# Late heads of a hybrid trunk: the norm factor's row, the decays and the last score take other places in the order

## The chip, the cores and the metric

The kernel runs on one core of a Trainium2 chip. The metric is device time in microseconds (us) of one execution. A core has five engines that work side by side, each through its own instructions in order: TensorE (PE in the profile, PEld for its weight loads), VectorE (DVE), ScalarE (ACT), GpSimd (POOL) and SyncE (SP), which here mostly issues DMAs. An instruction that waits holds up everything behind it on its engine.

## What is computed

The reference is a two-layer trunk on a sequence of 512 positions and 2048 features: an mLSTM layer of 8 heads, and then a band-attention layer. Both are modulated by a conditioning vector (the "ada" products). The change touches the mLSTM layer alone. Cut to that:

```python
proj = h @ w_in
qk = silu(causal_conv(proj[..., :A_V0], conv_w, conv_b))
v, o, z = proj[..., A_V0:A_O0], proj[..., A_O0:A_Z0], proj[..., A_Z0:A_G0]
gates = proj[..., A_G0:] + gate_b
ht = mlstm_chunkwise(heads(qk[..., :A_QK]), heads(qk[..., A_QK:]), heads(v), li, lf)
ht = rmsnorm(ht, g_head)
y = (sigmoid(o) * ht * silu(z)) @ w_out
```

Per head, `mlstm_chunkwise` is a causal attention without softmax: scores q·k are multiplied by decays, the exponential of a difference of gate sums, multiplied into the values and divided by a norm; then comes an RMS norm over the head's 512 columns.

## The kernel before

**Products and weights.** All products are in fp32 made of three products of split operands: x = hi + lo, both in the format that PE takes at full speed, and hi·hi + hi·lo + lo·hi. Weights stream from DRAM in numbered pieces of 128 rows by up to 1024 columns. SP loads piece i to `wr`i. ACT casts it to `wh`i (the hi part), then DVE subtracts it from the raw piece (the lo part, same tile): `split`, L243. Where a projection uses fewer products by a Strassen-like scheme, DVE first makes sums of the piece's blocks, `ws`i (L282 to L284, of which L283 writes into the raw piece, so that the cast of `wh`i waits for it), and these are split in turn into `wsh`i. So each piece of a late head costs ACT two casts and DVE five instructions, and PE multiplies `wh` and `wsh` against the activations `h1` and their sums `h1s`.

**Heads.** Heads 0 to 2 run beside the conditioning sums and the build-up of `h1s`. Heads 3 to 7 (h > `HALF`, the late heads) all run alike, 165.9 us each: a pair of projections for the queries (`proj_s` through `pair`, 4 pieces, in head 3 pieces 105 to 108), a pair for the keys (109 to 112), the values (`proj_v`, 8 pieces, 113 to 120), four pairs of output and gate projections (`ps_dzo` and so on, 16 pieces), and then norm, denominator and numerator of the head. Each projection of queries and keys goes through `conv`: an affine step on ACT, three multiply-adds on DVE (L793, written into `cv`), a silu on ACT (L796), and a split into `qk`. `proj_v` runs its 8 pieces (k = 0 to 7, n = 8) against two blocks of positions (b = 0, 1), whose banks `ps_d`, `ps_c`, `ps_a` and a shared `ps_e` are accumulated in PSUM; pieces 0 and 1 are held and run together, block 0 of both and then block 1 of both, and so are the last two, 6 and 7. Behind the last piece's block 0 `empty` reads that block's banks.

**Scores.** `scores(h, j)` for j = 0 to 3 is called amid the values pieces: six products into `ps_s`, two exponentials on ACT (L855, L857) into `e` (the decays; `e` tiles come from a pool that they share with others), a multiplication on DVE (L860) and a split into `p`; for j = 3 a single multiplication (L865). For j > 0 the result is added to a total (L870). Before, score 3 is called before piece 7 is fetched, so it stands on PE amid the held pieces.

**The norm factor's row.** The norm and square sum of a head are known at its end; `row_out` sends them to DRAM and `factor(h)` loads them back as a 16x32 tile `f` with DMAs on POOL (L886). The rest of it is deferred (`head_due`) into the next head: maximum (DVE, L890), square (ACT, L891), a multiply-add and a clamp (DVE, L892, L893), square root (ACT, L894), reciprocal (DVE, L895), then two DMAs on POOL (L896, L897) that spread the row over 128 partitions in `ssum`. Two of the instructions are tied behind `parted[0]`, the subtraction of the last weights piece at that point in the program. A second `head_due` amid the values multiplies the head's output rows by `ssum` (L904).

**What sets the order.** The program is given to a list scheduler, which orders each engine's instructions by priority: program order, moved forward by `tc.high_priority(lead)` by `lead` steps (`AHEAD` is 300). `behind(a, b)` adds an order without a semaphore. ACT keeps one set of function tables at a time; a switch of functions is an instruction of its own, ACT_TABLE_LOAD, under the line of the function that needs it.

Of the kernel before, what the change touches and what calls it, by code (L numbers as in the profile page):

```python
# [10 lines left out]
F32R = mybir.dt.float32r  # L11
AF = mybir.ActivationFunctionType
# [3 lines left out]
P = 128  # L16
D = 2048
S = 512
KT = D // P
NH = 8  # L20
DK = 256
DV = 512
INNER = 4096
V0 = 4096
# [9 lines left out]
AHEAD = 300  # L34
# [10 lines left out]
HEAD_PAIRS = 8  # L45
RAMP = [4, 5, 6, 7]
HALF = 2
# [140 lines left out]
def hybrid_trunk(ctx, tc, xT, xN, c, adaT, cols, wst, wg, ext, kc, out):  # L188
# [233 lines left out]
    def proj_v(mat, xs, ss, zs, name, pl, bufs, at={}):  # L422

        h0, h1_ = slice(0, 256), slice(256, 512)
        E = newp(f"ps_e{name}")
        banks = [[new(f"ps_{n}{name}_{b}") for n, new in zip("dca", news)] for b, news in enumerate(([newp] * 3, [newa, newp, newa]))]
        begun = set()
        n = KT // 2  # L430
        held = []

        def products(b, k, main, extra):
            D, C, A = banks[b]
            tok = slice(b * P, (b + 1) * P)
            for ps, half, parts, blk, x in (
                (D, 1, main, 1, ss[k][1]),
                (D, 0, main, 0, xs[2 * k][:, :, h0]),
                (C, 0, extra, 1, ss[k][2]),
                (C, 1, extra, 0, ss[k][0]),  # L440
                (A, 0, main, 3, xs[2 * k + 1][:, :, h0]),
                (A, 1, main, 2, ss[k][3]),
                (E, b, extra, 2, xs[2 * k + 1][:, :, h1_]),
            ):
                start = id(ps) not in begun
                begun.add(id(ps))
                w = slice(blk * 256, (blk + 1) * 256)
                last = k == n - 1 and (b if ps is E else ps is not D and half or ps is D and not half)
                mm3(ps[:, h1_ if half else h0], x[:, 0, tok], x[:, 1, tok], parts[0][:, w], parts[1][:, w], start, bool(last), 256)

        def empty(b):
            D, C, A = banks[b]
            z0, z1 = zs(b)
            f0, f1 = h0, h1_
            with tc.high_priority(AHEAD):
                nc.scalar.copy(z0[:, f0], D[:, h0])
                nc.vector.tensor_tensor(z1[:, f1], z0[:, f0], D[:, h1_], op=ALU.add)
                nc.vector.tensor_tensor(z1[:, f0], z1[:, f1], C[:, h0], op=ALU.add)
                nc.vector.tensor_tensor(z0[:, f1], z1[:, f1], C[:, h1_], op=ALU.add)
                nc.vector.tensor_tensor(z1[:, f1], z1[:, f0], C[:, h1_], op=ALU.add)  # L460
                nc.vector.tensor_tensor(z0, z0, A, op=ALU.add)
            return z0, z1

        out = []
        for k in range(n):
            if k in at:
                at[k]()
            held.append((k, *wpiece(mat, [2], pl, bufs)))
            if k in (0, n - 2):
                continue  # L470
            for b in range(2):
                for piece in held:
                    products(b, *piece)
                if k == n - 1:
                    out.append(empty(b))
            held.clear()
        for z, e in zip(out, (h0, h1_)):
            with tc.high_priority(AHEAD):
                nc.vector.tensor_tensor(z[1][:, h0], z[1][:, h0], E[:, e], op=ALU.add)
        return [z[a] for a in range(2) for z in out]  # L480
# [299 lines left out]
            nc.tensor.transpose(pt[:, j * 8 : j * 8 + 8], e[:, j * P : (j + 1) * P], ident[:8, :8])  # L780
        nc.vector.tensor_copy(aT.rearrange("p a b -> p (a b)"), pt[:, :32])

    def conv(ps, ch, name, first, woven):

        acc = tp.tile([P, S], F32, tag="t", name=f"cv_{name}")
        with tc.high_priority(AHEAD if first else 0):
            if woven:
                rows = tp.tile([P, S], F32, tag="t", name=f"cu_{name}")
                nc.scalar.copy(like(rows, S), read(ps, S))
# [2 lines left out]
            for d in range(1, 4):  # L792
                nc.vector.scalar_tensor_tensor(  # L793
                    acc[:, d:], ps[:, : S - d], col(CW + 32 * (3 - d) + ch), acc[:, d:], op0=ALU.mult, op1=ALU.add
                )
        nc.scalar.activation(acc, acc, AF.Silu)  # L796
        t = hp.tile([P, 2, S], F32R, tag="qk", name=f"qk_{name}", bufs=4)
        split(t[:, 0, :], t[:, 1, :], acc)
        return t

    def sums(ps, x, name, early=0, late=0):
# [41 lines left out]
    def scores(h, j, qk, pr, nm, nmd, tot):  # L843
# [8 lines left out]
        psn = read(ps[:, : S - t0], S - t0)  # L852
        e = tp.tile([P, S], F32, tag="t", name=f"e{h}_{j}")
        a = aT[:, j, h : h + 1]
        nc.scalar.activation(e[:, 0:P], nmd[:, j, :], AF.Exp, bias=a)  # L855
        if n > P:
            nc.scalar.activation(e[:, P:n], nm[:, P * (j + 1) :], AF.Exp, bias=a)  # L857
        if j < 3:
            with tc.high_priority(AHEAD):
                nc.vector.scalar_tensor_tensor(like(e[:, :n], n), psn, DK**-0.5, like(e[:, :n], n), op0=ALU.mult, op1=ALU.mult)  # L860
# [53 lines left out]
    for h in range(NH):  # L914
# [4 lines left out]
        for i in range(4):  # L919
            if h > HALF:  # L920
                if i % 2 == 0:
                    zs = pair((i // 2) * (V0 // 2) + h * DK, f"zq{h}_{i}", BANKS[i // 2], HEAD_PAIRS, {3: head_due} if i else {}, lead=AHEAD - 30 * i)
                ps = zs[i % 2]
            elif h < 2:
                ps = (lead, qk1)[h][i]
            else:
                ps = newp(f"ps_qk{h}_{i}")
                proj_a("a_w_in", h1, ps)
            qk.append(conv(ps, chs[i], f"{h}_{i}", 1 < h <= HALF, h in (0, HALF)))
            if 1 < h <= HALF:  # L930
                background(2)
                if i in (2, 3):
                    head_due()
# [30 lines left out]
        if h > HALF:  # L964
# [2 lines left out]
                t = [acp.tile([P, S], F32, tag="so", name=f"zv{h}_{b}_{a}", bufs=6) for a in range(2 - b)]  # L967
                return t + [hp.tile([P, S], F32, tag="nm", name=f"v{h}_3")] if b else t

            pv = proj_v("a_w_in", h1, h1s, rows_of, f"v{h}", hq, (2, 2), {k // 2: f for k, f in at.items()})  # L970
        else:
            pv = [newp(f"ps_v{h}_{m}") for m in range(4)]
            proj_b("a_w_in", h1, pv, at=at)
# [728 lines left out]
```

## Time and profile before

| | us |
|---|---|
| three runs | 2643.46 median, 2641.71 to 2646.48 |
| the profiled execution | 2643.82, its span 2642.1 |
| granted TensorE clock in it | 0.997 |
| ACT busy | 1436.6 |
| DMA | 193 GB/s in the mean |

The profile is a list of instructions with start, length, engine, line (L), operation, and tiles written <- read; in brackets stands the idle time of the engine just ahead and what ended it. Shown ends of instructions in a pipeline overlap the next one's start, so costs are read from start to start. The lines that carry the argument stand below.

### The profile page before, as it was taken

The page shows a single profiled execution, that of the slowest core. Times are in us where ns is not written, and L with a number is a line of the kernel's source. Part 1 is how long each engine was busy: PE and PEld are TensorE (multiplying, and loading weights), DVE is VectorE, ACT ScalarE, POOL GpSimd, SP SyncE. Part 2 cuts the span into 40 slices and gives each one's busy share as a digit, 9 for nine tenths or more (in the row PEclk, how much of TensorE's full clock was granted, in tenths as well). Part 3 has the DMA queues.
Part 4 walks back from the last instruction along what each step waited for, and adds up shares of the span by engine and source line. Part 5 has one row for each costly group of instructions (what it writes and reads, how often), then busy time and mean ns, then how long its engine had stood idle before and what let it go on. Part 6 is the DMA issues. An engine that isn't in the chain of part 4 may idle for free.

```text
span 2642.1 us, 45759 instructions
## 1 busy us (share of the span) xinstructions
PE 2575.3 (97%) x17994; PEld 2407.0 (91%) x17994; DVE 2335.6 (88%) x3812; ACT 1436.6 (54%) x2113; POOL 59.5 (2%) x118
## 2 busy tenths in 40 slices
PE   8999998999999999999999999999999999999998
PEld 6887887899999999999999898788999899999887
DVE  8978988999989999899998886977998999999767
ACT  4344533466556565565655443578543666676523
POOL 0000111000000000000000000000000000000000
PEclk9999999999999999999999999999999999999999
DMA  9776787533333323333246648888754544444787
GB/s 365 310 266 239 275 330 281 198 112 109 126 101 123 124 98 133 104 118 126 99 134 221 214 152 303 305 258 302 230 181 139 180 136 133 139 131 132 255 292 257
DMA packets 155314, 510.61 MB, mean 193 GB/s; under 512 B 17893, under 2 KB 31749, under 8 KB 140633
## 3 DMA queue, kind: packets, MB, share of 16 engines
q1 hardware_dynamic: 144346, 443.89, 49.1%
q0 software_dynamic: 10752, 63.79, 6.6%
q8 instruction: 141, 2.31, 0.4%
q14 instruction: 75, 0.61, 0.1%
HBM read 473.96 MB, written 38.90 MB: 194 GB/s over the span
## 4 chain that ended last, share of the span: by engine, by line
PE 56%; DVE 24%; issue 8%; DMA 6%; ACT 5%; POOL 0%; SPq 0%; DVEq 0%; ACTq 0%; POOLq 0%
DVE wh L243 6%; PE ps_y L311 5%; PE ps_dzo L311 4%; PE ps_czo L311 4%; PE ps_azo L311 4%; DVE ada L550 3%; PE ps_cz L311 3%; PE ps_dz L311 3%; PE ps_y_True L311 3%; PE ps_y_False L311 3%; PE ps_az L311 3%; DMA wr<-in_wst 2%; PE ps_bzo L311 2%; DVE wsh L243 2%; DVE cv L793 2%
## 5 line engine op out<-in xcount | busy, mean ns | idle before, releaser
L243 ACT CAST wh<-wr 128x1024 fp32r<-128x1024 f32 (+1 forms) x536 | 553.1, 1033 | 456.0 <-DVE wr L283 94.3
L243 DVE TENSOR_TENSOR wh<-wr,wh 128x1024 fp32r<-128x1024 f32 (+1 forms) x536 | 642.4, 1201 | 130.5 <-ACT wh L243 129.5
L243 ACT CAST wsh<-ws 128x768 fp32r<-128x768 f32 (+1 forms) x296 | 241.7, 817 | 308.5 <-PE ps_az L311 66.5
L243 DVE TENSOR_TENSOR wsh<-ws,wsh 128x768 fp32r<-128x768 f32 (+1 forms) x296 | 276.3, 933 | 49.1 <-ACT wsh L243 48.2
L550 DVE CUSTOM_DVE_ANT_0 ada<-ada,scB,cl 128x2048 f32<-128x2048 f32 (+1 forms) x89 | 205.7, 2320 | 12.5 <-DMA ada<-in_adaT 12.5
L282 DVE TENSOR_TENSOR ws<-wr 128x512 f32<-128x512 f32 (+1 forms) x296 | 197.6, 669 | 5.0 <-DMA wr<-in_wst 4.7
L311 PE MATMUL ps_y_False<-wh,y 128*128 128x512 f32 x768 | 168.4, 380 | 2.4 <-DVE wh L243 2.4
L311 PE MATMUL ps_y<-wh,y 128*128 128x512 f32 x768 | 168.6, 381 | 0.2 <-DVE wh L243 0.2
L311 PEld LDWEIGHTS ps_y_False<-wh,y 128*128 128x128 f32 x768 | 144.2, 189 | 24.4 <-DVE wh L243 4.3
L311 PEld LDWEIGHTS ps_y<-wh,y 128*128 128x128 f32 x768 | 144.3, 189 | 20.9 <-DVE wh L243 0.6
L311 PE MATMUL ps_v<-wh,h 128*128 128x512 f32 x576 | 129.2, 383 | 0.0
L311 PE MATMUL ps_kv<-wh,hkv 128*128 128x512 f32 x576 | 127.1, 381 | 1.7 <-DVE wh L243 0.9
L311 PEld LDWEIGHTS ps_kv<-wh,hkv 128*128 128x128 f32 x576 | 108.0, 189 | 18.4 <-DVE wh L243 2.4
L284 DVE TENSOR_TENSOR ws<-wr 128x256 f32<-128x256 f32 (+1 forms) x296 | 121.4, 412 | 3.4
L311 PEld LDWEIGHTS ps_v<-wh,h 128*128 128x128 f32 x576 | 109.4, 191 | 16.3 <-issue 0.9
L283 DVE TENSOR_TENSOR wr<-ws,wr 128x256 f32<-128x256 f32 (+1 forms) x296 | 121.0, 411 | 2.5
L311 PE MATMUL ps_l<-h,wh 128*128 128x512 f32 x480 | 107.8, 380 | 2.7 <-DVE wh L243 2.1
L311 PEld LDWEIGHTS ps_l<-h,wh 128*128 128x128 f32 x480 | 90.2, 189 | 17.4 <-DVE wh L243 3.3
L311 PE MATMUL ps_azo<-h,wh 128*128 128x256 f32 (+1 forms) x606 | 92.9, 285 | 0.0
L311 PE MATMUL ps_y_True<-wh,y 128*128 128x512 f32 x384 | 83.6, 380 | 0.3 <-ACT y L1250 0.3
L311 PEld LDWEIGHTS ps_y_True<-wh,y 128*128 128x128 f32 x384 | 72.5, 189 | 10.9 <-ACT y L1250 0.7
L311 PEld LDWEIGHTS ps_azo<-h,wh 128*128 128x128 f32 x606 | 79.3, 192 | 1.1
(432 smaller groups left out, 5827.2 us busy)
## 6 DMA issues: line engine op xcount, KB each, us to landing
wr<-in_wst SPq DMA_DIRECT2D x506, 512.0 KB, 3.7
ada<-in_adaT POOLq DMA_DIRECT2D x57, 1024.0 KB, 7.4
ada<-in_adaT SPq DMA_DIRECT2D x49, 1024.0 KB, 7.5
ada<-in_adaT SPq DMA_DIRECT2D x36, 512.0 KB, 6.7
wr<-in_wst SPq DMA_DIRECT2D x26, 384.0 KB, 5.3
xt<-nsc SPq DMA_DIRECT2D x32, 256.0 KB, 3.6
yr<-ysc SPq DMA_DIRECT2D x28, 256.0 KB, 5.3
ysc<-zo SPq DMA_DIRECT2D x24, 256.0 KB, 3.9
```

The source lines that it names most:

```text
L243: ins = nc.scalar.copy(hi, src), nc.vector.tensor_tensor(lo, src, hi.bitcast(F32), op=ALU.subtract)
L282: nc.vector.tensor_tensor(t[:, : 2 * w], r[:, w : 3 * w], r[:, : 2 * w], op=ALU.subtract)
L283: nc.vector.tensor_tensor(r[:, w : 2 * w], t[:, w : 2 * w], r[:, :w], op=ALU.add)
L284: nc.vector.tensor_tensor(t[:, 2 * w :], r[:, 3 * w :], r[:, w : 2 * w], op=ALU.subtract)
L311: product[0] = nc.tensor.matmul(ps, a, b, start=start, stop=stop)
L550: pin(nc.vector.tensor_tensor_reduce(c, c, (sc or scB)[:, j * w : (j + 1) * w], 1.0, mod[:, i : i + 1] if j else col(CB + i), ALU.mult, AL ...
L793: nc.vector.scalar_tensor_tensor(acc[:, d:], ps[:, : S - d], col(CW + 32 * (3 - d) + ch), acc[:, d:], op0=ALU.mult, op1=ALU.add)
```

## The change

Four things in the diff:

1. In late heads the deferred rest of the norm factor is called at step 1 instead of step 3 of the keys' pair of four pieces (`{1: head_due}`).
2. In `conv` the silu and the split of its result now stand inside the high-priority block. The parameter `first` becomes `lead`: `AHEAD` in head 2 as before, 100 for the keys of late heads, and 0 elsewhere.
3. In late heads the exponentials of `scores` are ordered behind the last convolution's silu (`silu[0]`).
4. `proj_v` calls the function due at step n behind block 0 of the last two pieces and their `empty`; score 3 of late heads is moved to that step.

```diff
@@ proj_v
                 if k == n - 1:
                     out.append(empty(b))
+                    if b == 0 and n in at:
+                        at[n]()
             held.clear()
@@
-    def conv(ps, ch, name, first, woven):
+    silu = [None]
+
+    def conv(ps, ch, name, lead, woven):
 
         acc = tp.tile([P, S], F32, tag="t", name=f"cv_{name}")
-        with tc.high_priority(AHEAD if first else 0):
+        with tc.high_priority(lead):
...
-        nc.scalar.activation(acc, acc, AF.Silu)
-        t = hp.tile([P, 2, S], F32R, tag="qk", name=f"qk_{name}", bufs=4)
-        split(t[:, 0, :], t[:, 1, :], acc)
+            silu[0] = nc.scalar.activation(acc, acc, AF.Silu)
+            t = hp.tile([P, 2, S], F32R, tag="qk", name=f"qk_{name}", bufs=4)
+            split(t[:, 0, :], t[:, 1, :], acc)
         return t
@@ scores
-        nc.scalar.activation(e[:, 0:P], nmd[:, j, :], AF.Exp, bias=a)
+        decays = [nc.scalar.activation(e[:, 0:P], nmd[:, j, :], AF.Exp, bias=a)]
         if n > P:
-            nc.scalar.activation(e[:, P:n], nm[:, P * (j + 1) :], AF.Exp, bias=a)
+            decays.append(nc.scalar.activation(e[:, P:n], nm[:, P * (j + 1) :], AF.Exp, bias=a))
+        if h > HALF:
+            for ins in decays:
+                behind(ins, silu[0])
@@ the loop over heads
-                    zs = pair(..., {3: head_due} if i else {}, lead=AHEAD - 30 * i)
+                    zs = pair(..., {1: head_due} if i else {}, lead=AHEAD - 30 * i)
...
-            qk.append(conv(ps, chs[i], f"{h}_{i}", 1 < h <= HALF, h in (0, HALF)))
+            qk.append(conv(ps, chs[i], f"{h}_{i}", AHEAD if h == HALF else 100 if h > HALF and i > 1 else 0, h in (0, HALF)))
...
-            pv = proj_v("a_w_in", h1, h1s, rows_of, f"v{h}", hq, (2, 2), {k // 2: f for k, f in at.items()})
+            pv = proj_v("a_w_in", h1, h1s, rows_of, f"v{h}", hq, (2, 2), {k // 2 + (k == KT - 2): f for k, f in at.items()})
```

DVE in the keys' pair of head 3, before (tile names carry the head and the piece, and behind those a running number of the tile):

```order
L243 TENSOR_TENSOR wh109_5045<-wr109_5039,wh109_5045 128x1024
L282 TENSOR_TENSOR ws110_0_5095<-wr110_5093 128x512
L283 TENSOR_TENSOR wr110_5093<-ws110_0_5095,wr110_5093 128x256
L284 TENSOR_TENSOR ws110_0_5095<-wr110_5093 128x256
L243 TENSOR_TENSOR wsh109_0_5048<-ws109_0_5041,wsh109_0_5048 128x768
L243 TENSOR_TENSOR wh110_5099<-wr110_5093,wh110_5099 128x1024
```

And with the change:

```order
L243 TENSOR_TENSOR wh109_5045<-wr109_5039,wh109_5045 128x1024
L282 TENSOR_TENSOR ws110_0_5103<-wr110_5101 128x512
L897 TENSOR_TENSOR f2_4782<-f2_4782 16x32
L283 TENSOR_TENSOR wr110_5101<-ws110_0_5103,wr110_5101 128x256
L899 SCALAR_TENSOR_TENSOR f2_4782<-f2_4782 16x32
L284 TENSOR_TENSOR ws110_0_5103<-wr110_5101 128x256
L900 TENSOR_SCALAR f2_4782<-f2_4782 16x32
L902 RECIPROCAL f2_4782<-f2_4782 16x32
L243 TENSOR_TENSOR wsh109_0_5048<-ws109_0_5041,wsh109_0_5048 128x768
L243 TENSOR_TENSOR wh110_5107<-wr110_5101,wh110_5107 128x1024
```

The four DVE steps of head 2's norm factor (`f2`; lines are seven higher in the changed kernel) now stand among pieces 109 and 110.

ACT in the values of head 3, before, where those steps stood until now:

```order
L791 ACTIVATE cv_3_3_5279<-zq3_2_1_5034,cl_100 128x512
L855 ACT_TABLE_LOAD
L855 ACTIVATE e3_0_5530<-nmd3_5289,aT_1513 128x128
L891 ACTIVATE f2_4782<-f2_4782 16x32
L857 ACTIVATE e3_0_5530<-nm3_5288,aT_1513 128x384
L243 CAST wh116_5475<-wr116_5469 128x1024
L243 CAST wsh115_0_5416<-ws115_0_5409 128x768
L894 ACT_TABLE_LOAD
L894 ACTIVATE f2_4782<-f2_4782 16x32
L243 CAST wsh116_0_5478<-ws116_0_5471 128x768
L796 ACT_TABLE_LOAD
L796 ACTIVATE cv_3_2_5270<-cv_3_2_5270 128x512
```

And with the change:

```order
L795 ACTIVATE cv_3_3_5279<-zq3_2_1_5034,cl_100 128x512
L243 CAST wh116_5475<-wr116_5469 128x1024
L243 CAST wsh115_0_5416<-ws115_0_5409 128x768
L243 CAST wsh116_0_5478<-ws116_0_5471 128x768
L800 ACTIVATE cv_3_2_5270<-cv_3_2_5270 128x512
```

The decays of score 0, the norm factor's square and root, and three loads of function tables are gone from this place.

PE in the last two values pieces of head 3, before (pieces 119 and 120, block 0):

```order
L311 MATMUL ps_av3_0_5295<-wh119_5681,h1_13_1127 128x256 x3
L311 MATMUL ps_s3_3_5687<-qk_3_0_5021,qk_3_2_5276 128x256 x3
L311 MATMUL ps_s3_3_5687<-qk_3_1_5030,qk_3_3_5285 128x256 x3
L311 MATMUL ps_av3_0_5295<-wh119_5681,h1s6_42_4300 128x256 x3
L311 MATMUL ps_ev3_5292<-wsh119_0_5684,h1_13_1127 128x256 x3
```

And with the change:

```order
L311 MATMUL ps_av3_0_5295<-wh120_5693,h1_15_1314 128x256 x3
L311 MATMUL ps_av3_0_5295<-wh120_5693,h1s7_42_4530 128x256 x3
L311 MATMUL ps_ev3_5292<-wsh120_0_5696,h1_15_1314 128x256 x3
L311 MATMUL ps_s3_3_5749<-qk_3_0_5021,qk_3_2_5276 128x256 x3
L311 MATMUL ps_s3_3_5749<-qk_3_1_5030,qk_3_3_5285 128x256 x3
L311 MATMUL ps_dv3_1_5296<-wh119_5681,h1s6_42_4300 128x256 x3
```

Score 3 of head 3 stood amid piece 119 of block 0; it now stands between block 0 and block 1 of both pieces.

More of the change, by code (lines that the diff above doesn't have):

```diff
@@ L921, in hybrid_trunk @@
                 if i % 2 == 0:
-                    zs = pair((i // 2) * (V0 // 2) + h * DK, f"zq{h}_{i}", BANKS[i // 2], HEAD_PAIRS, {3: head_due} if i else {}, lead=AHEAD - 30 * i)
+                    zs = pair((i // 2) * (V0 // 2) + h * DK, f"zq{h}_{i}", BANKS[i // 2], HEAD_PAIRS, {1: head_due} if i else {}, lead=AHEAD - 30 * i)
                 ps = zs[i % 2]
```

## The prediction

> **What bounds the kernel now.** I read the page first, then the groups of matmuls with the wait ahead of each, then the windows and the rows of one late head. From the page, the span and the busy row:
>
> ```profile
> span 2642.1 us, 45759 instructions
> PE 2575.3 (97%) x17994; PEld 2407.0 (91%) x17994; DVE 2335.6 (88%) x3812; ACT 1436.6 (54%) x2113; POOL 59.5 (2%) x118
> ```
>
> PE is busy 97% of the span, so only about 67 us exist that a reordering could win, and of those only what lies where the change works. The changed heads are 3 to 7. Two groups of their matmuls carry a wait (behind the second bar: idle time ahead, and its releaser):
>
> ```profile
> L311 PE MATMUL ps_cv<-wsh,h1s 128*128 128x256 f32 x240 | 42.1, 279 | 8.8 <-DVE wsh L243 8.8
> L311 PE MATMUL ps_s<-qk,qk 128*128 128x256 f32 x96 | 14.5, 282 | 7.3 <-DVE e L860 7.3
> ```
>
> Over five heads that is 8.8 / 5 = 1.8 us and 7.3 / 5 = 1.5 us a head. PE's rows around the two waits of head 3, whose values run from 637.23 to 681.84:
>
> ```profile
> 647.46 0.28 PE L311 MATMUL ps_cv<-wsh,h1s 128*128 128x256 f32 x1
> 649.49 0.49 PE L311 MATMUL ps_cv<-wsh,h1s 128*128 128x256 f32 x2 [1.75 <-DVE wsh L243]
> ...
> 671.85 0.50 PE L311 MATMUL ps_av<-wh,h 128*128 128x256 f32 x3
> 673.36 0.94 PE L311 MATMUL ps_s<-qk,qk 128*128 128x256 f32 x6 [1.01 <-DVE e L860]
> ...
> 675.47 0.50 PE L311 MATMUL ps_cv<-wsh,h1s 128*128 128x256 f32 x3
> ...
> 681.84 0.83 PE L311 MATMUL ps_dzo<-h1s,wh 128*128 128x256 f32 x6
> ```
>
> Groups of three products start 0.335 us apart where nothing waits (so 0.112 us each; shown ends overlap). From start to start the first wait loses 649.49 − 647.46 − 0.112 = 1.92 us and the second 673.36 − 671.85 − 0.335 = 1.18 us: 3.1 us a head, 15.5 us in five. Behind 675.47 nothing waits: 19 groups of 0.335 make the 6.37 us to 681.84. Now what stands behind both waits (length, then busy time and instructions of PE, PEld, DVE, ACT, POOL; clock, DMA share, GB/s):
>
> ```profile
> 615.00:649.40 34.40, 32.74 (x292) 32.44 (x290) 34.36 (x61) 21.99 (x31) 0.00 (x0) 1.00 0.27 93
> 649.40:671.00 21.60, 21.51 (x184) 21.35 (x185) 21.57 (x37) 13.77 (x21) 1.56 (x3) 1.00 0.63 215
> 637.20:681.80 44.60, 41.83 (x362) 41.19 (x362) 42.61 (x78) 28.56 (x41) 1.56 (x3) 1.00 0.41 139
> ```
>
> **VectorE is the bound of this stage**: 34.36 of 34.40 us and 21.57 of 21.60, while ACT is busy for two thirds. PE outruns DVE through keys and values and waits for whichever split weights DVE has not finished. So I count what DVE no longer does between 615 and the last piece of the values (piece 120), not what ACT saves.
>
> **The change part by part.** *The row of the norm factor.* Its instructions now stand on DVE and ACT at 612 to 615, not at 643 to 650. DVE and ACT there before:
>
> ```profile
> 612.31 0.42 DVE L283 TENSOR_TENSOR wr<-ws,wr 128x256 f32<-128x256 f32 x1
> ...
> 614.22 0.96 DVE L243 TENSOR_TENSOR wsh<-ws,wsh 128x768 fp32r<-128x768 f32 x1 [1.02 <-ACT wsh L243]
> ```
>
> ```profile
> 613.36 0.83 ACT L243 CAST wsh<-ws 128x768 fp32r<-128x768 f32 x1 [2.94 <-issue]
> ```
>
> The same instructions where they stood until now, first on DVE and then on ACT:
>
> ```profile
> 642.97 0.17 DVE L890 TENSOR_TENSOR f<-f 16x32 f32<-16x32 f32 x1
> 643.08 0.73 DVE L793 SCALAR_TENSOR_TENSOR cv<-zq,cl,cv 128x511 f32<-128x511 f32 x1
> ...
> 645.07 0.17 DVE L892 SCALAR_TENSOR_TENSOR f<-f 16x32 f32<-16x32 f32 x1
> 645.17 0.73 DVE L793 SCALAR_TENSOR_TENSOR cv<-zq,cl,cv 128x509 f32<-128x509 f32 x1
> 645.83 0.16 DVE L893 TENSOR_SCALAR f<-f 16x32 f32<-16x32 f32 x1
> 645.91 1.52 DVE L793 SCALAR_TENSOR_TENSOR cv<-zq,cl,cv 128x511 f32<-128x511 f32 x2
> ...
> 649.35 0.33 DVE L895 RECIPROCAL f<-f 16x32 f32<-16x32 f32 x1
> 649.62 0.61 DVE L282 TENSOR_TENSOR ws<-wr 128x512 f32<-128x512 f32 x1
> ```
>
> ```profile
> 644.13 0.21 ACT L891 ACTIVATE f<-f 16x32 f32<-16x32 f32 x1
> ...
> 646.54 1.28 ACT L894 ACT_TABLE_LOAD   x1
> 647.83 0.23 ACT L894 ACTIVATE f<-f 16x32 f32<-16x32 f32 x1
> 647.97 0.81 ACT L243 CAST wsh<-ws 128x768 fp32r<-128x768 f32 x1
> ```
>
> From start to start the row costs DVE 0.11 (643.08 − 642.97) + 0.10 + 0.08 + 0.27 (649.62 − 649.35) = 0.56 us; that leaves the saturated stretch. In its new place the first three fall into DVE's idle 1.02 us before 614.22. On ACT the chain is late: the maximum starts at about 612.31, the square runs to about 612.65, the table load takes 1.28 (to 613.93), the root 0.14 to the next start, so the cast of wsh109, at 613.36 until now, begins at about 614.08. ACT had been idle 2.94 us ahead of it, which hides the rest; 614.08 − 613.36 = 0.72 is not hidden. The reciprocal fits into DVE's longer idle time. DVE therefore starts its part of wsh109 0.72 to 0.73 us later, and from there has no gap to make that up in. So far 0.56 − 0.73 = −0.17 us: **this part alone loses a little**.
>
> A sentence on a price that no row here bears: the Trainium skill, "ScalarE: Activation LUTs", section "What ACT_TABLE_LOAD costs", gives a switch of tables about 1283 ns of load and 1380 ns of drain, 2.66 us in all. The trace agrees with the load (1.28) and shows no drain behind it: the load at 646.54 ends at 647.82 and the root starts at 647.83. By the page's figure the cast would begin at about 615.46, the sum of this head would fall by 1.38 us, and nothing would be won (the second rival's outcome).
>
> *The last score and its decay.* In the order of before ACT computes score 3's decay ahead of the next weights' cast, and PE the score itself in the middle of piece 119. DVE and then ACT there:
>
> ```profile
> 670.17 0.42 DVE L283 TENSOR_TENSOR wr<-ws,wr 128x256 f32<-128x256 f32 x1
> ...
> 671.75 1.22 DVE L243 TENSOR_TENSOR wh<-wr,wh 128x1024 fp32r<-128x1024 f32 x1 [0.70 <-ACT wh L243]
> ...
> 673.22 0.95 DVE L243 TENSOR_TENSOR wsh<-ws,wsh 128x768 fp32r<-128x768 f32 x1
> 674.09 0.42 DVE L243 TENSOR_TENSOR p<-e,p 128x256 fp32r<-128x256 f32 x1
> ```
>
> ```profile
> 670.67 1.05 ACT L243 CAST wh<-wr 128x1024 fp32r<-128x1024 f32 x1
> ```
>
> DVE idles 0.70 us for the cast of wh121, which cannot start before L283 is done at about 670.58. In the new order the addition of a decayed score (L877, a 128x384 form, 0.47 us from start to start) stands between L283 and that wait instead of ahead of it, and the decay no longer precedes the cast on ACT (0.1 us). Some 0.4 of the 0.70 us is filled; bounds 0 and 0.70, and I take 0.4 since the cast's own 1.05 us stays. wsh120 is then complete on DVE at 674.09 + 0.73 − 0.56 − 0.4 = 673.86.
>
> PE: score 3 (six products, 0.67 us) now stands behind block 0 of pieces 119 and 120, so its slot in PSUM has 3.0 us more (nine groups of 0.335) to come free and the wait of 1.18 for score 2's DVE step is gone. What is late next is wsh120: PE would reach its first product (675.47 before) at 675.47 − 0.67 − 1.18 − 0.2 to 0.5 (from the first wait) = 673.1 to 673.4 and waits until 673.86. From there on PE's work is the same 6.37 + 0.67 us, so the output products start at 673.86 + 7.04 = 680.90, against 681.84: **0.94 us a head**. The first wait, for wsh115, shrinks by 0.2 to 0.5 (a third convolution step, 0.66, also moves behind wsh115), but what it gives is eaten at wsh120.
>
> Bounds of a head: 0, if the root or the cast eats the rest, and 3.1, if both waits go. Five heads at 0.94: 4.7 us.
>
> *Silu and split of the convolutions under high priority; decays behind the last silu.* In late heads these are orders on engines with the same instructions; seven table loads fewer in all (113 for 120) are ACT time, and ACT is no bound: nothing. In heads 0 and 1 the scheduler's order changes (the subtractions for split weights come behind conditioning sums, some scores come earlier). I expect new PE waits of 1 to 3 us each there and others gone, some 2 us late in all at the end of head 1's gate. What takes that:
>
> ```profile
> 412.83 2.35 DVE L550 CUSTOM_DVE_ANT_0 ada<-ada,scB,cl 128x2048 f32<-128x2048 f32 x1 [0.62 <-DMA ada<-in_adaT]
> ...
> 418.04 1.28 DVE L1047 TENSOR_TENSOR so<-ps_n,so 128x512 f32<-128x512 f32 x2
> ```
>
> ```profile
> 418.78 3.61 PE L311 MATMUL ps_n<-p,v 128*128 128x512 f32 x11 [4.41 <-DVE so L1047]
> ```
>
> PE waits 4.41 us there for a DVE instruction at the end of a row of sums that wait for their own DMA (0.62). PE arriving 2 us late is covered by the 4.41; if that cover went, it would cost those 2. I take 0, bounds −1 (fewer sums ahead of L1047, one is 2.35) and +3.
>
> Sum: −4.7 + 0 = −4.7 against the profiled execution of 2643.82 (span 2642.1 and 1.7 around it): 2639.1. The median of the three runs, 2643.46, is 0.36 lower, and so would give 2638.8. I say **2639.0**.
>
> **The rivals.**
>
> *Both waits go (0.13).* If ACT's switches of tables, not DVE's work, hold back the casts that DVE follows, then fewer switches free both: 11 to 15.5 us, 2628 to 2632. For it: DVE's only two gaps around (1.02 and 0.70) both end with ACT. Against it: 34.36 of 34.40 us without any gap between them.
>
> *The root's chain costs what it saves (0.17).* The earlier root delays wsh109's cast. Each 0.1 us more on ACT is lost one for one on DVE; at 0.94 more, that is a cast at 615.0, nothing is won: 2643.5, between 2641 and 2646. (The page's drain of 1.38 us, above, would do that; the rows show none.) For it: the chain alternates DVE, ACT, DVE, ACT, DVE, each handover behind other work. Against it: 2.94 us of idle time on ACT ahead.
>
> *Slower: DVE blocked by the row's reload (0.08).* The maximum now stands at about 612.3 on a DVE that runs in order, and every weight split is queued behind it. The row goes through DRAM and back on POOL's queue (the second line: median issue to landing):
>
> ```profile
> 608.60 0.48 POOL L886 DMA_DIRECT2D f<-dsc  x1 [3.34 <-DMA dsc<-row]
> ```
>
> ```profile
> f<-dsc POOLq DMA_DIRECT2D x14, 2.0 KB, 1.8
> ```
>
> 608.60 + 0.48 + 1.8 = 610.9, 1.4 us ahead of the need. A landing later than 613 costs one for one, and from about 614.0 the head is slower than before; for 0.2% (5.3 us, about what a measurement of this kernel can tell from no change) all five heads would need 615.0, 4 us late: 2646 to 2650. Against it: the margin.
>
> *The decays aren't moved* is no rival: the order of instructions shows that they are.
>
> **How the numbers follow.** Forecast 0.62, the rivals 0.13, 0.17 and 0.08. The forecast's own spread is 0.4 to 1.3 us a head (the filled idle time from 0 to 0.7) with −1 to +3 from heads 0 and 1: 2636 to 2644. Low end 2631, in the first rival's lower half; high end 2646, all but the last rival. 0.2% below the median is 2638.2: of the forecast's 0.62 some 0.27 lies below it, with the first rival's 0.13 that is faster 0.40. Slower takes 0.06 of the last rival and 0.01 of the forecast, 0.07; the same is the rest, 0.53.
>
> **What would show it.** In the changed profile, in each late head: the wait of ps_s for e is gone; a wait of 0.3 to 0.8 us stands ahead of ps_cv of the last piece, released by DVE's wsh; DVE is still without idle time through the values; the root's table load stands at 612.6 with the next cast at 614.1; values-start to first output product is 43.7 us for 44.6. Wrong would be: the first wait gone too (rival one), the wsh109 subtraction past 615.5 (rival two), an idle DVE ahead of the row's maximum (rival three), or PE waits between 205 and 425 us that the 4.41 us does not swallow.

## The result and the profile after

The changed kernel takes 2638.42 us in the median of 22 runs (2632.55 to 2641.18), the kernel before 2642.91 us in 22 runs beside it (2635.94 to 2648.66). The ratio is 0.9981, with a 95% interval of 0.9976 to 0.9987: 4.5 us less in the medians, 3.4 to 6.3 us by the interval. The forecast was 2639.0. The page's span and busy row:

```profile
span 2633.4 us, 45758 instructions
PE 2574.4 (98%) x17994; PEld 2407.5 (91%) x17994; DVE 2335.1 (89%) x3812; ACT 1428.7 (54%) x2106; POOL 59.8 (2%) x118
```

DVE's busy time is the same (2335.1 for 2335.6 us): the change moves work, it saves none of it. ACT has 7 instructions less, the table loads. The two groups that carried the waits, after:

```profile
L311 PE MATMUL ps_cv<-wsh,h1s 128*128 128x256 f32 x240 | 42.6, 280 | 9.8 <-DVE wsh L243 9.8
L311 PE MATMUL ps_s<-qk,qk 128*128 128x256 f32 x96 | 13.9, 278 | 0.0
```

The scores' wait of 7.3 us is gone (five times 1.01 us in the late heads, and 2.25 us at 260.81, ahead of them), and the split weights' wait has grown by 1.0 us. PE's rows around them in head 3, whose values now start at 633.72:

```profile
643.79 0.28 PE L311 MATMUL ps_cv<-wsh,h1s 128*128 128x256 f32 x1
645.62 0.49 PE L311 MATMUL ps_cv<-wsh,h1s 128*128 128x256 f32 x2 [1.56 <-DVE wsh L243]
...
669.66 0.28 PE L311 MATMUL ps_cv<-wsh,h1s 128*128 128x256 f32 x1
670.33 0.49 PE L311 MATMUL ps_cv<-wsh,h1s 128*128 128x256 f32 x2 [0.40 <-DVE wsh L243]
...
677.36 0.83 PE L311 MATMUL ps_dzo<-h1s,wh 128*128 128x256 f32 x6
```

From start to start the first wait loses 645.62 − 643.79 − 0.11 = 1.72 us (1.92 before), and the second, now for the last piece's sums, 0.56 us (1.18 before, for the score). From the first values product to the first output product are 677.36 − 633.72 = 43.64 us for 44.61. The experiments are read with this **values length** and with the **period**, the time from one late head's first output product to the next one's: 165.93 us before, 164.95 after. From head 4 on both repeat within 0.05 us in most kernels (the first period is 0.1 longer), while whole executions of one kernel differ by 5 to 17 us in the sets of ten or more.

Five periods give 5 × 0.98 = 4.9 us. The two profiled spans differ by 8.7; of that 637.23 − 633.72 = 3.5 us lie ahead of head 3's values, in the part that the experiments show to vary by itself (below).

DVE with the norm factor's row in its new place, and ACT beside it:

```profile
608.67 0.17 DVE L897 TENSOR_TENSOR f<-f 16x32 f32<-16x32 f32 x1
...
610.68 0.34 DVE L902 RECIPROCAL f<-f 16x32 f32<-16x32 f32 x1 [0.92 <-ACT f L901]
611.40 0.96 DVE L243 TENSOR_TENSOR wsh<-ws,wsh 128x768 fp32r<-128x768 f32 x1 [0.38 <-ACT wsh L243]
```

```profile
609.12 1.28 ACT L901 ACT_TABLE_LOAD   x1
610.42 0.23 ACT L901 ACTIVATE f<-f 16x32 f32<-16x32 f32 x1
610.55 0.81 ACT L243 CAST wsh<-ws 128x768 fp32r<-128x768 f32 x1
```

Counted from the start of the values, DVE begins wsh109 22.32 us ahead (633.72 − 611.40) instead of 23.01 (637.23 − 614.22): 0.69 us late, for an expected 0.73. The root starts 0.02 us after its table load ends. The drain that the Trainium skill adds to a load ("ScalarE: Activation LUTs", section "What ACT_TABLE_LOAD costs") shows here no more than before.

DVE at the end of the values, and the cast of wh121 on ACT:

```profile
666.26 0.42 DVE L283 TENSOR_TENSOR wr<-ws,wr 128x256 f32<-128x256 f32 x1
666.60 0.55 DVE L877 TENSOR_TENSOR e<-e,e 128x384 f32<-128x384 f32 x1
...
667.85 1.22 DVE L243 TENSOR_TENSOR wh<-wr,wh 128x1024 fp32r<-128x1024 f32 x1 [0.37 <-ACT wh L243]
669.00 0.42 DVE L867 SCALAR_TENSOR_TENSOR e<-ps_s,e 128x256 f32<-128x256 f32 x1
669.33 0.95 DVE L243 TENSOR_TENSOR wsh<-ws,wsh 128x768 fp32r<-128x768 f32 x1
670.20 0.42 DVE L243 TENSOR_TENSOR p<-e,p 128x256 fp32r<-128x256 f32 x1
```

```profile
666.76 1.06 ACT L243 CAST wh<-wr 128x1024 fp32r<-128x1024 f32 x1 [2.35 <-DVE wr L283]
```

The addition to the total (L877) now stands between L283 and wh121. The idle time ahead of wh121 is 0.37 us (0.70 before), and wsh120 starts 35.61 us behind the values' start for 35.99: 0.38 us earlier.

### The profile page after: what moved, and what is told of

It is laid out like the page before. It is cut to its first block, busy times and chain, and to the rows that moved or that the text cites. A ratio compares the mean times of both kernels' runs of the same rounds, so it can differ in the third digit from the quotient of the medians.

```text
span 2633.4 us, 45758 instructions
## 1 busy us (share of the span) xinstructions
PE 2574.4 (98%) x17994; PEld 2407.5 (91%) x17994; DVE 2335.1 (89%) x3812; ACT 1428.7 (54%) x2106; POOL 59.8 (2%) x118
## 4 chain that ended last, share of the span: by engine, by line
PE 56%; DVE 25%; DMA 8%; issue 7%; ACT 3%; POOL 0%; SPq 0%; DVEq 0%; ACTq 0%; POOLq 0%
DVE wh L243 6%; PE ps_y L311 5%; PE ps_azo L311 4%; PE ps_czo L311 4%; PE ps_dzo L311 4%; DVE ada L552 3%; PE ps_y_True L311 3%; PE ps_dz L311 3%; PE ps_cz L311 3%; PE ps_y_False L311 3%; PE ps_az L311 3%; DMA wr<-in_wst 3%; DVE wsh L243 2%; PE ps_bzo L311 2%; DVE cv L797 2%
## 5 line engine op out<-in xcount | busy, mean ns | idle before, releaser
L282 DVE TENSOR_TENSOR ws<-wr 128x512 f32<-128x512 f32 (+1 forms) x296 | 198.5, 673 | 5.3 <-DMA wr<-in_wst 5.0
L284 DVE TENSOR_TENSOR ws<-wr 128x256 f32<-128x256 f32 (+1 forms) x296 | 122.1, 414 | 3.1
L283 DVE TENSOR_TENSOR wr<-ws,wr 128x256 f32<-128x256 f32 (+1 forms) x296 | 121.8, 413 | 2.4
```

Of the source, the lines that this page charges most:

```text
L282: nc.vector.tensor_tensor(t[:, : 2 * w], r[:, w : 3 * w], r[:, : 2 * w], op=ALU.subtract)
L283: nc.vector.tensor_tensor(r[:, w : 2 * w], t[:, w : 2 * w], r[:, :w], op=ALU.add)
L284: nc.vector.tensor_tensor(t[:, 2 * w :], r[:, 3 * w :], r[:, w : 2 * w], op=ALU.subtract)
```

## Experiments

All kernels are read by values length and period, and by time where several runs were made. First each part of the change by itself, and all but one.

**Score 3's place alone.** The edit, on the kernel before:

```diff
                 if k == n - 1:
                     out.append(empty(b))
+                    if b == 0 and n in at:
+                        at[n]()
...
-            pv = proj_v(..., {k // 2: f for k, f in at.items()})
+            pv = proj_v(..., {k // 2 + (k == KT - 2): f for k, f in at.items()})
```

> The kernel before with the place of score 3 alone changed. Length of a late head here: from the first values product on PE to the first output product, 44.6 us before (637.23 to 681.84) and 43.6 us with the whole change. Theory (DVE is the bound; the gain is score 3 and its decay out of the way of the last pieces): 43.5 us, 1.1 us less; no wait of ps_s for e, a last wait of ps_cv for wsh below 0.4 us, the first wait still about 1.9 us. Rival 1 (ACT's switches of tables are what the whole change removes): 44.5 us or more, since no switch goes. Rival 2 (the parts only work together): 44.0 to 44.4.

Values 44.02 us, period 165.34: 0.59 us less, half of what was expected, and no table load fewer (one execution: 2638.62, beside 2643.86 before). The wait for the score is gone, the first wait stands at 1.92, and a new one of 0.59 us stands ahead of wsh120. DVE and then ACT ahead of it, in head 5:

```profile
999.73 0.55 DVE L872 TENSOR_TENSOR e<-e,e 128x384 f32<-128x384 f32 x1
1000.20 0.41 DVE L283 TENSOR_TENSOR wr<-ws,wr 128x256 f32<-128x256 f32 x1
...
1001.77 1.22 DVE L243 TENSOR_TENSOR wh<-wr,wh 128x1024 fp32r<-128x1024 f32 x1 [0.70 <-ACT wh L243]
```

```profile
1000.37 0.40 ACT L857 ACTIVATE e<-nmd,aT 128x128 f32<-128x128 f32 x1 [1.90 <-DVE e L872]
1000.69 1.05 ACT L243 CAST wh<-wr 128x1024 fp32r<-128x1024 f32 x1
```

DVE still idles 0.70 us ahead of the next piece's wh (wh121 in head 3), since the total's addition (L872 here) still stands ahead of L283 and not behind it. Score 3's decay (L857) is not the cause: the cast starts 0.49 us behind L283 with the decay ahead of it (1000.69 − 1000.20), and 0.50 us behind it without, in the changed kernel (666.76 − 666.26). That score 3's place is worth something by itself was right, the size was not. The 44.02 us lie in the second rival's range, 44.0 to 44.4; what speaks against that rival is that the same 0.6 us comes back on top of the other two parts, below.

**The norm factor's row alone.** `{3: head_due}` becomes `{1: head_due}` in the kernel before, nothing else.

> The kernel before with the norm factor's row alone moved to step 1 of the keys' pair. Theory (DVE is the bound): the row's root delays wsh109 on DVE by 0.7 us and takes 0.56 us out of the saturated stretch, so 44.7 to 44.9 us instead of 44.6; the wait for wsh115 gets much shorter (the order now puts it 3.6 us of other DVE work earlier), but the time comes back in later waits. Rival 1 (switches of tables): the root's switch is gone from the values, so the first wait's 1.3 to 1.9 us are kept: 42.7 to 43.3 us.

Values 46.0 us, period 167.3 (one execution: 2646.74): slower by 1.4 us, more than any theory had. The first wait did shrink to 0.36 us, as the order said. What came back was not the root's 0.17 us. PE around score 0 of head 5, and ACT there:

```profile
994.12 0.39 PE L311 MATMUL ps_cv<-wsh,h 128*128 128x256 f32 x2
996.30 0.70 PE L311 MATMUL ps_s<-qk,qk 128*128 128x512 f32 x2 [1.79 <-ACT qk L243]
```

```profile
993.67 1.28 ACT L796 ACT_TABLE_LOAD   x1
994.97 0.63 ACT L796 ACTIVATE cv<-cv 128x512 f32<-128x512 f32 x1
995.63 0.62 ACT L243 CAST qk<-cv 128x512 fp32r<-128x512 f32 x1
```

The last key's convolution had slipped behind other DVE work, so its silu (with a table load, since decays stood ahead of it) and split came just as PE needed them. Behind the wait PE then ran slowly; the windows of the trace around it (columns as in the prediction's windows):

```profile
985.00:994.20 9.20, 9.20 (x82) 9.12 (x81) 9.20 (x16) 7.12 (x9) 0.00 (x0) 1.00 0.55 181
994.20:998.00 3.80, 1.90 (x9) 1.40 (x9) 3.80 (x7) 3.69 (x5) 0.00 (x0) 0.91 0.63 204
998.00:1000.70 2.70, 2.70 (x14) 2.67 (x13) 2.50 (x5) 0.94 (x2) 0.00 (x0) 0.50 0.65 241
1000.70:1006.00 5.30, 5.30 (x46) 5.30 (x46) 4.15 (x7) 2.17 (x4) 0.00 (x0) 0.99 0.38 136
```

The granted clock is 0.50 for 2.7 us: 14 products where 24 of 128x256 would fit at 0.112 us, some 1.1 us lost in this window alone. How much of the 1.4 us this makes, and why it came, the run of the row with score 3's place shows (below).

**The convolutions alone.** The silu and split under high priority and the decays behind the last silu, on the kernel before:

```diff
         with tc.high_priority(lead):
...
-        nc.scalar.activation(acc, acc, AF.Silu)
-        t = hp.tile(...)
-        split(t[:, 0, :], t[:, 1, :], acc)
+            silu[0] = nc.scalar.activation(acc, acc, AF.Silu)
+            t = hp.tile(...)
+            split(t[:, 0, :], t[:, 1, :], acc)
...
+        if h > HALF:
+            for ins in decays:
+                behind(ins, silu[0])
```

> The kernel before with the convolutions' silu and split under high priority and the decays behind the last silu, alone; the row and score 3 stay. Theory (DVE is the bound and has the same work): 44.4 to 44.8 us. Rival 1 (switches of tables): one or two switches a head go here, so 43.3 us or less.

Values 47.1 to 49.4 us, period 170.4 to 170.7: slower by 4.5 us or more a head (2661.24 in one execution), with as few table loads as the changed kernel (113). Both theories fell. DVE and POOL in the values of head 5 (started 977.52):

```profile
999.24 0.33 DVE L900 RECIPROCAL f<-f 16x32 f32<-16x32 f32 x1
...
1007.73 1.29 DVE L909 TENSOR_TENSOR zo<-zo,ssum 128x512 f32<-128x512 f32 x2 [3.24 <-DMA ssum<-dsc]
```

```profile
999.87 0.48 POOL L901 DMA_DIRECT2D dsc<-f  x1 [52.61 <-DVE f L900]
1003.78 0.57 POOL L902 DMA_DIRECT2D ssum<-dsc  x1 [3.43 <-DMA dsc<-f]
```

With the silu and the splits ahead of it, the row's last step came 21.7 us into the values (before, in the same head: reciprocal at 981.33, 12.1 us in). The way through DRAM takes 8.5 us from the reciprocal to the first multiplication, which held DVE for 3.24 us in the midst of the weights. PE lost 0.98 us and then 3.37 us behind it and was granted a clock of 0.56 from 1016.5 to 1019.6, behind the longer wait. Head 3 has nearly the same waits (2.88 us for ssum) and no lowered clock: 47.1 us. So the late ssum costs about 2.5 us, and most of the rest comes with the clock.

**All but the row.** The changed kernel with `{3: head_due}`.

> The changed kernel with the norm factor's row back at step 3 of the keys' pair. Theory: the row's move costs 0.73 us on DVE and gives 0.56, so without it a head is 0.1 to 0.2 us shorter than the changed kernel's 43.64: 43.4 to 43.6 us. Rival 1 (switches of tables): the switch for the root is back among the values' casts, so 44.0 us or more.

Values 46.7 to 49.4 us, period 168.0 to 170.9 (2661.33 in one execution): the rival's side of the forecast, and for neither theory's reason. DVE waits 3.21 us for ssum in head 6, as in the last kernel. Heads 5 and 6 have the same waits, 3.19 and 3.21 us for ssum, and take 46.69 and 48.31 us: in head 6 the granted clock is 0.50 for 3.41 us (from 1189.76), in head 5 it stays at 1.00. One such stretch at half clock thus costs 1.6 us here. So my first reading, that the row's move costs a little and the rest brings the gain, was wrong: **the row's move is what the convolutions' priority needs**. I formed a second theory: each of the two opens a wait that the other closes.

**Row and convolutions, without score 3's place.** The changed kernel with `k // 2` and without the call behind `empty`.

> The changed kernel with score 3 back at its old place, so the row's move and the convolutions' priority with the decays behind them, together. The runs so far give a late head's values 44.61 us before, 43.64 with the whole change, 44.02 with score 3 alone, 46.0 with the row alone (keys late: PE waits 1.96 us for qk) and 47 to 49 with the convolutions alone (DVE waits 3.24 us for the norm factor's ssum). New theory: these two parts each open a wait that the other closes, and together they take 0.38 us off, the amount by which DVE's multiplication for score 2 is earlier in the changed kernel; score 3's place gives the other 0.6. So 44.2 us, a wait of ps_s for e of about 1.1 us, and no wait of DVE for ssum. Rival: the parts do not add up like that, and without the place of score 3 the head is no shorter than before, 44.6 or more.

Values 44.21 to 44.23 us, period 165.53 (one execution: 2639.32), as expected: PE waits 1.14 us for DVE's multiplication of score 2, and DVE waits for no ssum. The second theory holds: apart the two cost 1.4 and 4.5 us a head, half clock included, and together they save 0.40.

**Row and score 3's place, without the convolutions' part.** Silu, split and decays as in the kernel before.

> The changed kernel with the convolutions' silu and split at their old priority and the decays free, so the row's move and score 3's place together. New theory: the late split of the last key (qk) stays the wait that decides, since score 0 needs it: PE waits 1.5 to 2.0 us for qk, and the values take 45.3 to 46.0 us. Rival: score 3's place relieves the end by its full 0.6 to 1.2 us and hides the wait, 44.8 or less.

Values 44.04 to 44.08 us, period 165.38 (one execution: 2644.33). The wait for qk is there (1.98 us), as expected, yet the head is 1.9 us shorter than with the row alone and shorter than my 45.3. Its clock stays at 1.00 behind that wait. Most of the difference is thus the half clock, which the row alone met and this kernel did not. By the traces it turns on where the wait falls. In the row's kernel the clock goes to 0.50 at 662.84, 830.10, 997.35, 1164.60 and 1331.86 us, for 3.41 us each time. These are 167.25 us apart, 49 times 3.413, and in every trace of this case all changes of the clock are whole multiples of 3.413 us apart. Head 5 of the row's kernel in stretches of that length:

```profile
993.94:997.35 3.41, 1.60 (x11) 1.16 (x9) 3.41 (x7) 3.35 (x4) 0.00 (x0) 1.00 0.57 169
997.35:1000.76 3.41, 3.32 (x14) 3.23 (x15) 3.15 (x7) 1.60 (x4) 0.00 (x0) 0.50 0.71 269
```

And head 5 of this kernel, in its own:

```profile
990.69:994.10 3.41, 2.48 (x23) 2.29 (x21) 3.41 (x7) 2.80 (x3) 0.00 (x0) 1.00 0.67 255
994.10:997.51 3.41, 2.44 (x16) 2.17 (x17) 3.41 (x7) 1.81 (x4) 0.00 (x0) 1.00 0.53 158
```

In the first the wait for qk falls whole into one stretch of 3.41 us; in the second two stretches share it. The row's kernel has a period of 167.28 us, almost the 49 stretches, so its five heads all fall the same way; whether that match is chance is open. With 165.38 us each head falls another way. The busy time that the profile gives draws no sharp line: the stretches ahead of the five half clocks have 9 to 11 products, and two in heads 4 and 6 of this kernel have 13, at about the same busy time (1.61 and 1.59 us), and no half clock follows. Without a half clock, and beside score 3's place, the row's move costs next to nothing: 165.38 us for 165.34 with score 3's place alone.

**Heads 0 and 1 in the order of before.** The edit moves silu and split out of the block of high priority where `lead` is 0:

```diff
-            silu[0] = nc.scalar.activation(acc, acc, AF.Silu)
...
-        return t
+            if lead:
+                return done(acc, name)
+        return done(acc, name)
```

`done` holds the three lines taken out. It reaches further than I had said: the late heads' queries have lead 0 too.

> The changed kernel with the silu and split of heads 0 to 1 ahead of the block of high priority again, which gives these heads the order of before. Theory: the stage from 205 to 425 us is paced by the DMA of the conditioning sums, so its order is worth nothing: values 43.6 us a late head, time within 2 us of the changed kernel's 2638.4 (2636.4 to 2640.5), ratio to before 0.9975 to 0.9990. Rival: the new order of heads 0 and 1 is worth the 3.5 us that the two profiled executions differ in there: about 2642, ratio 0.9995 or more.

2634.86 us (10 runs), ratio 0.9980 (0.9971 to 0.9989): within the theory's ratios, 1.5 us below its lower time, and far from the rival's 2642. The late period is 164.76 (values 43.12), 0.19 less, through the queries. For heads 0 and 1 the start of head 3's values in all profiles decides: with the order of before 637.23, 636.44, 636.09, 638.65, 635.15 and 638.19, mean 637.0; with the changed order 633.72, 636.42, 638.38, 640.47, 638.03, 639.90, 637.17 and 634.23, mean 637.3. The order of heads 0 and 1 is worth nothing that these show.

**The root off ACT.** From head 2's factor on, the square on DVE and the root and reciprocal as a power on POOL:

```diff
-            nc.scalar.activation(n, n, AF.Square, scale=EPS**0.5)
+            nc.vector.scalar_tensor_tensor(n, n, EPS, n, op0=ALU.mult, op1=ALU.mult)
...
-            nc.scalar.activation(n, n, AF.Sqrt)
-            nc.vector.reciprocal(n, n)
+            nc.gpsimd.memset(m, -0.5)
+            nc.gpsimd.tensor_tensor(n, n, m, op=ALU.pow)
```

> The changed kernel with, from head 2's norm factor on, the square as a DVE multiplication and the root and reciprocal as one power of -0.5 on GpSimd, so no switch of tables for it on ACT ahead of wsh109. Theory: the cast of wsh109 is 0.7 us earlier again, DVE's saturated stretch begins 0.7 us earlier, and the values take 42.9 to 43.1 us a head for 43.64: about 2635, ratio to before 0.996 to 0.9975. Rival 1: the last piece is then held by something else than DVE's work and the head stays at 43.6, 2638. Rival 2: GpSimd's power is so slow, or slows DVE beside it so much, that ssum is late and DVE waits for it: 44 us a head or more, 2640 or more.

Values 43.40 us, period 164.73: 0.22 less, a third of what was expected (2636.45 us in 12 runs, ratio 0.9980, 0.9970 to 0.9989). The first link is as predicted; the last is not:

```profile
616.89 0.96 DVE L243 TENSOR_TENSOR wsh<-ws,wsh 128x768 fp32r<-128x768 f32 x1 [0.74 <-ACT wsh L243]
...
673.79 1.23 DVE L243 TENSOR_TENSOR wh<-wr,wh 128x1024 fp32r<-128x1024 f32 x1 [0.70 <-ACT wh L243]
```

wsh109 begins 23.01 us ahead of the values (start 639.90), exactly as before the change: the 0.69 us are back. But the scheduler put the total's addition ahead of L283 again (and score 3's decay ahead of the cast of wh121, which is not later for it: 0.49 us behind L283), and DVE idles 0.70 us there instead of 0.37. That gives back 0.33 of the 0.69; where the other 0.14 went I did not trace.

**Root off ACT, and the decay and the total's addition out of the way.** On top of the last kernel:

```diff
+                if j == 3:
+                    behind(ins, pcast[0])
...
-            split(t[:, 0, :], t[:, 1, :], e[:, :n])
+            pcast[0] = split(t[:, 0, :], t[:, 1, :], e[:, :n])[1]
...
+        if h > HALF and j == 1:
+            later.append(add)
+            return
+        while later and j == 3:
+            later.pop(0)()
```

`add` is the addition to the total.

> root_off_act with two more steps out of the way of the last piece: score 3's decay is ordered behind the cast of score 2's product on ACT, and the addition of score 1 to the total is called with score 3 instead of with score 1. From one head's first output product to the next head's it was 165.93 us before, 164.95 with the change, 164.73 in root_off_act, where PE still waits 0.5 us for wsh120. Theory (that wait is the DVE work and the cast ahead of wsh120): DVE has 0.47 us less ahead of it and the cast is free 0.1 us earlier, so the wait goes from 0.5 to below 0.1 us and the period is 164.2 to 164.35; three quarters of a us a head less than the changed kernel, about 2635. Rival: what is freed only lengthens DVE's idle time for the cast of wh121, and the period stays at 164.6 to 164.75.

The four periods are 164.60, 164.49, 164.69 and 164.48 us (165.08, 164.97, 164.95 and 164.94 with the change), values 43.16: 0.25 less than in the last kernel but for one head, half of the expected and between the theory's range and the rival's; the wait for wsh120 went from 0.50 to 0.25 us, and DVE's idle time ahead of wh121 to 0.79. Time 2635.44 us in 11 runs, ratio to before 0.9970 (0.9960 to 0.9981), beside 2640.14 for the changed kernel on the same chip. It beats both kernels by its period, 1.45 us a head less than before and 0.47 less than the change.

**The rows' multiplications on POOL.** On top of that, `scaled` with `nc.gpsimd` for heads 2 to 6, and there without the tie behind `parted[0]`.

> root_decay with the four multiplications of the previous head's output rows by the norm factor on GpSimd instead of DVE, 0.61 us of DVE each, 2.4 us a head, all behind the first wait and ahead of the last. Theory: the last wait is gone already, so a head gains nothing more there (period 164.1 to 164.4), while DVE shows 1 to 2.4 us of idle time before the last piece; the first wait stays at 1.5 to 1.7 us since this work was behind it. Rival: GpSimd's multiplications slow DVE's own instructions or hold the rows so long that the period grows to 164.7 or more.

Period 171 to 174 us, 2670.41 us in 4 runs, ratio 1.0112 (1.0092 to 1.0133): the rival, and stronger than it said. POOL, DVE and SP's queue in head 5:

```profile
962.24 7.50 POOL L929 TENSOR_TENSOR zo<-zo,ssum 128x512 f32<-128x512 f32 x4 [2.60 <-DMA ssum<-dsc]
```

```profile
961.64 0.42 DVE L284 TENSOR_TENSOR ws<-wr 128x256 f32<-128x256 f32 x1
...
965.42 1.49 DVE L283 TENSOR_TENSOR wr<-ws,wr 128x256 f32<-128x256 f32 x1
966.83 1.77 DVE L797 SCALAR_TENSOR_TENSOR cv<-zq,cl,cv 128x510 f32<-128x510 f32 x1
968.53 1.50 DVE L284 TENSOR_TENSOR ws<-wr 128x256 f32<-128x256 f32 x1
...
975.53 0.69 DVE L282 TENSOR_TENSOR ws<-wr 128x512 f32<-128x512 f32 x1 [3.98 <-DMA wr<-in_wst]
```

```profile
964.98 5.11 SPq L932 DMA_DIRECT2D ysc<-zo  x4
970.20 7.52 SPq L259 DMA_DIRECT2D wr<-in_wst  x3
```

Two things happen. Four of DVE's instructions take 1.0 to 1.1 us longer while POOL multiplies (L284: 0.42 and 1.50). And the stores of these rows, which wait for POOL in SP's queue, stand ahead of the next weights' loads: those are issued from 970.20 on, and DVE waits 3.98 us for them.

**The changed kernel again.**

> The changed kernel itself beside these on the same chip: period 164.95 us, about 2638.4, ratio to before 0.9975 to 0.9990. All theories say so; its profile also gives a second sample of the stage of heads 0 and 1, where the first values product of head 3 started at 633.7 us in the one profile of this kernel and at 635 to 640 us in the others. Theory (that stage is paced by DMAs and scatters): the start lies between 634 and 641 us. Rival: 633.7 is this kernel's own, and it lies within 0.5 us of that.

Period 164.97, values 43.64; 2640.14 us (12 runs), ratio 0.9991 (0.9981 to 1.0001). Head 3's values start at 636.42, 2.7 us from the first profile of the same kernel: the 633.72 was one sample of a part that varies. The ratio is just outside the expected 0.9975 to 0.9990 and its interval reaches 1: with 12 runs beside 22 the times alone do not tell this kernel from the one before, while the period does.

**Root, decay, and the queries' steps at their old priority.** The edit of heads01_as_before on top of root_decay.

> root_decay with the silu and split of all convolutions but the late keys' (and head 2's) at the old priority, as in heads01_as_before: there that edit, which also put the late queries' steps back, took the period from 164.95 to 164.76 us, a shorter wait for wsh115 against a new one of 0.2 us in the first output pair. Theory (DVE work is shifted behind wsh115): the same 0.15 to 0.2 us again, period 164.25 to 164.4 us for root_decay's 164.48; about 2634.5, ratio to before 0.9960 to 0.9980. Rival: the last wait is down to 0.25 us already, what is shifted behind wsh115 comes back at wsh120 or in the output pair, and the period is 164.45 or more.

Period 164.79, 0.3 longer than without the edit, so the rival: the first wait is 1.51 (1.59), the last one 0.44 (0.25). 2634.99 us in 11 runs, ratio 0.9976 (0.9967 to 0.9985), which can't be told from root_decay's. The gain of 0.19 that the same edit had in the changed kernel does not carry over.

## Why the prediction was right, and where it was not

The forecast of 0.94 us a head, 4.7 in all, was measured as 0.98 and 4.9 by the period, and as 4.5 in the medians (2.4 in the second set of runs, 2640.14 beside 2642.55); the sum's terms:

| term, a head of the changed kernel | forecast | measured |
|---|---|---|
| wsh109 on DVE later | 0.73 | 0.69 |
| DVE's idle time ahead of wh121 | 0.3 of 0.70 left | 0.37 left |
| wsh120 done on DVE earlier | 0.23 | 0.38 |
| first wait shorter by | 0.2 to 0.5 | 0.20 |
| PE's new wait for wsh120 | 0.45 to 0.75 | 0.56 |
| values length | 43.7 | 43.64 |
| heads 0 and 1 | 0 (−1 to +3) | no difference seen |

That the sum came so close is in part luck. wsh120 was done 0.15 us earlier than forecast (0.38 for 0.23), from a source that is not traced. Against that PE began with it 0.13 us behind the start of DVE's next instruction (670.33 − 670.20), the mark that the sum took for its end, with nothing for the handover. And the 0.1 us for the decay ahead of the cast is not there: the cast starts 0.50 us behind L283 with the decay and without it (670.67 − 670.17 before, 666.76 − 666.26 after), so the addition alone filled the idle time, by 0.33 us.

*DVE bounds the stage, and PE's end is set by the last split weights.* Right: the wait that replaced the score's is for wsh120, released by DVE. The reading of the group's row, 7.3 / 5 = 1.5 us a head, was wrong, since 2.25 of the 7.3 us lie ahead of the late heads; the sum went by the rows, 1.18 us, and is not touched by it.

*Heads 0 and 1 give nothing* held in the way that was told. Of PE's waits there the 2.25 us at 260.81 are gone, one for qk grew from 2.70 to 4.37 us, and the 4.41 us ahead of ps_n, which were to swallow the difference, fell to 1.31.

*Both waits go* fell: the first stays at 1.7 us with seven table loads fewer, and score 3's place gains 0.59 us a head with none fewer. *The root's chain costs what it saves* did not occur: the load shows no drain, and the cast comes 0.7 us late, not 2.1. *DVE blocked by the row's reload* did not occur at the place where I put it; DVE runs into the maximum without a wait. A block of that kind is real, though: it stands at the other end of the row, at ssum, in the kernels without the row's move.

What was wrong is the account by parts. The step on the row, "this part alone loses a little", and the step on the convolutions, "ACT is no bound: nothing", priced each part inside the order of the whole change. Alone, the row costs 1.4 us and the convolutions 4.5 us a head. In both the scheduler's order opens a new wait, for a late qk and for a late ssum, and a half clock worth about 1.6 us follows it (in all heads but head 3 of the convolutions' kernel). Without the half clock the row's move is near the small loss that was forecast (0.04 us beside score 3's place, for 0.17), but by another way: PE's wait for qk takes the place of its first wait. For the convolutions "nothing" stays wrong, by about 2.5 us. The pair gives 0.40, and score 3's place 0.58 more on top of it, which is the total. The sum came out because it was made on the changed kernel's own order, not by adding the parts.

## What to carry to other kernels

Where one engine is saturated through a stage, count what the new order puts ahead of the last thing that the waiting engine needs; the first wait's size says little, since a later one takes it up. A part of a change that looks like a loss may pay for another: take out one part at a time from the whole before calling it useless, and look for who then waits. Read the granted clock behind each wait before pricing a part by its time: here two heads with equal waits lay 1.6 us apart by it. A row that goes through DRAM needs its lead time (here 8.5 us) ahead of its first reader on a saturated engine.

## What the runs showed of the hardware

A granted clock of 0.50 followed waits well short of a long stop. The Trainium skill, "TensorE: Matmul & The Clock Gate", section "What's actually happening", has the clock halved after an idle window of about 3.4 us; here PE was not idle through such a window. In the row's kernel the longest wait was 1.96 us, stretches of 3.41 us with PE busy for 1.51 to 1.62 us (9 to 11 products) went ahead, and the clock was 0.50 for the next 3.41 us. Behind stretches with 1.59 and 1.61 us (13 products) in the kernel with the row and score 3's place it stayed at 1.00. The clock changed at whole multiples of 3.413 us alone, so that one and the same wait was followed by a half clock or not by where it fell.

POOL's multiplication of 128x512 took 1.88 us in the mean (7.50 / 4) where DVE takes 0.60, and four DVE instructions that overlapped them took about 1.05 us longer; L282 at 963.12, beside the first of them, kept its 0.69 us. The Trainium skill, "SBUF — State Buffer", section "SBUF: two separate sides", says that the two share a pair of ports as an exclusive lock when the DVE instruction has two inputs in SBUF; the four stretched instructions are of that kind, and the trace agrees as far as they go. One power on a 16x32 tile took POOL 5.45 us.
